# A weight stream split in two parts: the low part of every second chunk by an accumulating transfer

## The chip, the cores and the metric

The kernel runs on one core of one Trainium2 chip. The metric is the device time of one execution in microseconds. A profile of one execution stands beside it; all times in this text come from that profile or from the timed runs.

## What is computed

One layer of a decoder block for 256 tokens of width 2048, in float32: a norm, one wide projection, two branches (dilated attention, a gated recurrence), a gated merge, a mixing product with a norm and a residual, and a gated feed-forward part with a norm and a residual. Cut to what matters:

```python
D_MODEL, SEQ, D_FF = 2048, 256, 5632
a = rmsnorm(x, norm_mix_pre)
proj = a @ w_in                                   # 2048 x 17408
q_a, k_a, v_a, q_r, f_r, i_r, g_r, gate_a, gate_r = split_columns(proj)
attn = ...    # three groups of 8 heads, windows of stride 1, 4, 16, mixed by their denominators
r_out = ...   # HGRN2: S_t = diag(f_t) S_{t-1} + k_t v_t^T, o_t = S_t^T q_t; norm; gate
y = sigmoid(gate_a) * (attn @ w_attn_branch) + sigmoid(gate_r) * (r_out @ w_hgrn_branch)
h = x + rmsnorm(y @ w_mix_out, norm_mix_post)
a = rmsnorm(h, norm_ffn_pre)
gt, up = split(a @ w_ffn_gate_up)                 # 2048 x 11264
out = h + rmsnorm((silu(gt) * up) @ w_ffn_down, norm_ffn_post)
```

## The kernel before

All weights pass through one stream of 600 chunks in the order of the products. A chunk is a tile of 128 partitions by 1024 float32, 512 KB. The products are done at near float32 precision on TensorE by splitting each operand in two parts: a high part, which is the number rounded to TensorE's float32r format, and a low part, which is what the rounding left. Three products (high by high, high by low, low by high) make one.

For each chunk j there are four steps:

1. `load(j)` (L191) issues the transfer from HBM into a tile `raw` on the queue of SP, the sync engine. There are six `raw` buffers.
2. `split(j)` (L206) makes `wh` on ScalarE, a copy that rounds (L221), and then `wl = raw - wh` on VectorE (L222). `wh` and `wl` have three buffers each, except for the last four chunks (`HELD`), which have tiles of their own.
3. `multiply(j)` (L224) issues the matrix products of the chunk on TensorE into `acc` banks of PSUM, of which there are four; a block of columns uses two. It comes in three kinds: N with the activations stationary, T and W with the weights stationary.
4. After the last chunk of a block, its evacuation (`evac`) is put in a queue. It is a generator that is advanced by one step per chunk, on ScalarE, VectorE and partly GpSimd.

The order of the instructions on each engine is the order in which they are written; no scheduler moves them. The main loop (L1116) does for each chunk i: `split(i + 2)`, `load(i + 8)`, `multiply(i)`, and then one step of the evacuations and of two lanes of side work. The lanes hold the attention heads, the recurrence and the second norm. So a split is written two chunks ahead of its use, and the buffers that it writes are those that chunk i - 1 has used last.

GpSimd's queue holds the recurrence's products and differences (L605, L612, L635, L643, L663, L666, L676, L688) and five pieces of the first residual (L874); for the rest of the time it is empty. No transfer is issued on it.

Of the kernel before, what the change touches and what calls it, by code (L numbers as in the profile page):

```python
# [16 lines left out]
AF = mybir.ActivationFunctionType  # L17
OP = mybir.AluOpType
# [18 lines left out]
N_RAW, N_SPLIT, AHEAD, HELD, WARM, BRIDGE = 6, 3, 2, 4, 8, 6  # L37


class Block:  # L40
    """Columns of one product: how they are computed, their operands, and what follows.

    N: 512 columns, activations stationary: tokens on partitions, one bank for 128 tokens.
    T: 512 columns, weights stationary: columns on partitions, two times 128 of them a bank.
    W: 256 columns, weights stationary, both parts of the activations in one stream: 128
       columns a bank, whose halves have yet to be added.
    """

    def __init__(self, kind, w, nk, col, xs, evac, parity=False, pre=None, mid=None, post=None):
        self.kind, self.w, self.nk, self.col = kind, w, nk, col  # L50
# [9 lines left out]
def tile_hybrid_block(ctx: ExitStack, tc: tile.TileContext, t, out):  # L60
    nc = tc.nc
# [3 lines left out]
    stream = ctx.enter_context(tc.tile_pool(name="stream", bufs=1, reuse_waits="tile"))  # L65
# [25 lines left out]
        nc.tensor.matmul(ps, lhsT, rhs, start=start, stop=stop, skip_group_check=True)  # L91

    def rsqrt_mean(dst, ss, n, bias=None):
        """dst = (ss / n + bias) ** -0.5, with a Newton step behind the tables.

        bias: columns with the bias and with -0.5 times it.
        """
        w = ss.shape[-1]
        v, y, a = (small(s)[:, :w] for s in ("v", "y", "a"))
        bias = bias or (eps[:, 0:1], eps[:, 1:2])  # L100
        nc.scalar.activation(y, ss, AF.Ln, scale=1.0 / n, bias=bias[0])
        nc.scalar.activation(y, y, AF.Exp, scale=-0.5)
        nc.vector.tensor_scalar(v, ss, -0.5 / n, bias[1], op0=OP.mult, op1=OP.add)
        if w == 1:
            nc.vector.scalar_tensor_tensor(out=a, in0=y, scalar=v, in1=y, op0=OP.mult, op1=OP.mult)
        else:
            nc.vector.tensor_mul(a, y, y)
            nc.vector.tensor_mul(a, a, v)
        nc.vector.scalar_tensor_tensor(
            out=dst, in0=a, scalar=1.5, in1=y, op0=OP.add, op1=OP.mult  # L110
        )

# [1 line left out]
    warm = cpool.tile([P, 512], mybir.dt.bfloat16, name="warm")  # L114
    nc.vector.memset(warm, 0.0)
    ones = cpool.tile([P, P], F32, name="ones")
# [38 lines left out]
    lb = kp.tile([P, 8], F32, name="lb")  # L155
    lb1 = kp.tile([P, 8], F32, name="lb1")

# [1 line left out]
    blocks, chunks = [], []  # L159

    def add(*args, **kw):
# [23 lines left out]
        return go  # L185

    def parts(j):
        """The first chunk goes in two parts: the arithmetic starts sooner."""
        return (slice(0, 512), slice(512, 1024)) if j == 0 else (slice(0, 1024),)

    def load(j):  # L191
# [14 lines left out]
    def split(j, only=None):  # L206
        if j >= len(chunks):
            return
        raw = chunks[j][2]
        if chunks[j][3] is None:  # L210
            if j < len(chunks) - HELD:
                chunks[j][3:] = [
                    stream.tile([P, 1024], F32R, tag=s, bufs=N_SPLIT, name=nm(s))
                    for s in ("wh", "wl")
                ]
            else:
                chunks[j][3:] = [rslot(s) for s in ("wh", "wl")]
        wh, wl = chunks[j][3:]
        for n, k in enumerate(parts(j)):
            if only in (None, n):  # L220
                nc.scalar.activation(wh[:, k], raw[:, k], AF.Copy)  # L221
                nc.vector.tensor_sub(wl[:, k], raw[:, k], wh[:, k].bitcast(F32))  # L222

    def multiply(j, sides=(0, 1)):  # L224
        b, c = chunks[j][:2]
# [30 lines left out]
                    mm(ps, h, xl, False, False)  # L256
                    mm(ps, l, xh, False, last)

# [1 line left out]
    class Split:  # L260
        """Two K-tiles a slot, each with its high and low part for the 256 tokens."""

        def __init__(self, s, nk, slot=rslot):
            self.flat = [slot(s) for _ in range(nk // 2)]
# [8 lines left out]
            return self(k)[0].bitcast(F32)  # L273

        def put(self, n, src):
            """Both K-tiles of slot n from [128, 2, 256]."""
            x = self.slots[n]
            nc.scalar.activation(x[:, :, 0, :], src, AF.Copy)
            nc.vector.tensor_sub(x[:, :, 1, :], src, x[:, :, 0, :].bitcast(F32))

    def transpose_in(src, gcol, dst, c, apart=False):
        """Two K-tiles of dst from [token, feature] pieces, times a gain by feature."""
        ps = []
        for k in (2 * c, 2 * c + 1):
            if apart or not ps:
                bank = aux()
            ps.append(bank[:, :S] if apart else bank[:, (k % 2) * S : (k % 2 + 1) * S])
            for b in range(2):
                nc.tensor.transpose(  # L289
                    ps[-1][:, b * P : (b + 1) * P],  # L290
                    src[k // 4][:, b, (k % 4) * P : (k % 4 + 1) * P],
                    ident,
                )
        def high(kk):
            k = 2 * c + kk
            nc.scalar.activation(dst(k)[0], ps[kk], AF.Copy, scale=gcol[:, k : k + 1])  # L296

        def low(kk):
            k = 2 * c + kk
            nc.vector.scalar_tensor_tensor(  # L300
                out=dst(k)[1], in0=ps[kk], scalar=gcol[:, k : k + 1],
                in1=dst.f32(k), op0=OP.mult, op1=OP.subtract,
            )

        if apart:
            return high, low
        high(0), high(1), low(0), low(1)

    def row_broadcast(dst, rc):
        """dst[p, t] = rc[t % 128, t // 128] for every p."""  # L310
        ds = [small("diag", P, 2) for _ in range(2)]
        for b in range(2):
            nc.vector.tensor_scalar(ds[b], ident, rc[:, b : b + 1], None, op0=OP.mult)
        yield
        ps = aux()
        for b in range(2):
            mm(ps[:, b * P : (b + 1) * P], ones[:, :P], ds[b], True, True)
        yield
        nc.scalar.activation(dst, ps[:, :S], AF.Copy)
# [16 lines left out]
        while q:  # L336
            advance(q)

# [1 line left out]
    xt = [hslot("x") for _ in range(4)]  # L340
    xv = t["x"][0].rearrange("(b p) c -> p b c", p=P)
    xT = Split("xT", KD)
# [67 lines left out]
        nc.sync.dma_start(lmask, t["lmask"])  # L410

    def keep_warm(n):
        """Products of no use, so that the tensor engine's clock doesn't fall in a wait."""
        ps = aux()
        for _ in range(n):
            mm(ps, warm[:, :P], warm, True, True)
# [15 lines left out]
        if c + 2 < KD // 2:  # L432
            transpose_in(xt, colg, xT, c + 2)

# [1 line left out]
    fT, qT, gN, iN = {}, {}, {}, {}  # L436

    def evac_f(half):
# [60 lines left out]
    qkT, vN = {}, {}  # L499

    def evac_rope(key, tab, then=None):
        """Rotary positions; the tokens leave with the even ones before the odd ones."""
        cos = tabs[:, tab, :]
        sin = tabs[:, tab + 1, :]

# [19 lines left out]
                then()  # L525
        return ev

# [1 line left out]
    attnT = Split("attnT", 8)  # L529
    recT = Split("recT", 8)  # L530

# [44 lines left out]
        )  # L576
        yield

# [1 line left out]
    def recurrence(half):  # L580
        q, f, g = qT[half], fT[half], gN[half]
        q = q.rearrange("p h t -> p (h t)")
# [44 lines left out]
            )  # L627

        def level64():
            """64 tokens against the 64 before them."""  # L630
            x = fslot("x")
            xe, be, ke, qe = (
                a.rearrange("p (e c t) -> p e c t", e=8, c=2) for a in (x, b, kk, q)
# [18 lines left out]
            )  # L652

        def level128():
            """The second 128 tokens against the first."""
            x = fslot("x")
            xc, bc = (a.rearrange("p (h c t) -> p h c t", h=4, c=4) for a in (x, b))
            end = small("end")
# [24 lines left out]
            nc.scalar.activation(a2[0], ps, AF.Copy)  # L683

        def same():
            """A token against itself."""
            x = fslot("x")
            nc.gpsimd.tensor_mul(x, q, kk)  # L688
            yield
# [63 lines left out]
            recT.put(2 * half + j, ps.rearrange("p (h t) -> p h t", h=2))  # L753
            yield

# [1 line left out]
    gates = {}  # L757
    waiting, heads_done = [], [False]

# [26 lines left out]
    part = {}  # L786
# [20 lines left out]
            yT[0].put(2 * j + i, src)  # L807
        return ev

# [1 line left out]
    zg, hx, gpost, zss = {}, {}, [], []  # L811
    h_t, hT = {}, []

# [39 lines left out]
        )  # L853

    def so_far(ss):
        """By side: mean plus eps of the first three of four parts, and -0.5 times it."""
        b = small("base")
        nc.vector.tensor_reduce(
            b[:, :2], ss.rearrange("p (b j) -> p b j", b=2)[:, :, :3], op=OP.add,
# [29 lines left out]
        residual_of(2, False)  # L889

    def residual_of(m, spread=True):
        """The columns behind the K-tiles of chunk m."""
        residual(m // 2, m % 2 * 256, m % 2 * 256 + 256, spread=spread)

    def mid_ffn():
# [78 lines left out]
    def act(k):  # L974
        return act_t[k // 2](k % 2)

# [1 line left out]
    fss, fz, fpost = [], {}, []  # L978

    def begin_down():  # L980
# [40 lines left out]
        return zpool[0].tile([P, 2, 512], F32, tag="z", bufs=4, name=nm(s))  # L1021

    def finish(i):
        """The last tokens of side i: norm, residual, store."""
        sq, r3 = fss[0][:, 4 * i + 3 : 4 * i + 4], r3c[:, i : i + 1]

        def store(j, lo=0, hi=512, eng=nc.sync):
# [13 lines left out]
        down_side(3, i, blocks[-1].banks[i], others)  # L1041
        store(3)

# [1 line left out]
    w_in = t["w_in"][0]  # L1045

    def start_recurrence():
# [97 lines left out]


def _tables():
    """Rotary tables and masks: they depend on shapes alone."""
    inv = (10000.0 ** (-np.arange(0, HD, 2) / HD)).astype(np.float32)
    ang = (np.arange(S, dtype=np.float32)[None, :] * inv[:, None]).astype(np.float64)  # L1150
    cos, sin = np.cos(ang), np.sin(ang)
# [4 lines left out]
    j = np.arange(P)  # L1156
# [31 lines left out]
```

## Time and profile before

| | |
|---|---|
| runs | 1780.1 and 1778.14 us, median 1779.12 |
| span of the profiled execution | 1779.4 us |
| TensorE busy, with 9579 products | 1764.4 us (99%) |
| VectorE busy, 1331 instructions | 1098.2 us (62%) |
| ScalarE busy, 1166 instructions | 846.8 us (48%) |
| GpSimd busy, 54 instructions | 74.1 us (4%) |
| moved by the DMA engines | 326.08 MB, on average 183 GB/s |
| share of the 16 DMA engines taken by SP's queue | 55.6% |

The profiled execution's span is within 0.3 us of the median of the runs, so its rows can be summed against the time directly. In the profile, busy times are sums of instructions by engine; "idle before, releaser" is the time an engine stood idle ahead of a group of instructions and what ended that idle time; the time to landing of a transfer runs from its issue to the arrival of its data.

### The profile page before, as it was taken

The numbers are of one execution on the slowest core, as the hardware profiler recorded it, in microseconds if no ns is written. First come the engines' busy times: TensorE is split into PE (matmuls) and PEld (weight loads), VectorE is DVE, ScalarE is ACT, GpSimd is POOL, SyncE is SP. The second block draws the span as 40 slices with busy tenths as digits, with TensorE's granted clock in tenths as the row PEclk, the third lists the DMA queues.
The fourth block names the chain that finished last, engine by engine and source line by source line (L and its number), as shares of the span: only waits on it lengthen the run. The fifth ranks groups of instructions, "written<-read, shape, count | busy, mean of one in ns | idle before, by whom it ended". The sixth has DMA issues, their size and how long they took to land.

```text
span 1779.4 us, 24318 instructions
## 1 busy us (share of the span) xinstructions
PE 1764.4 (99%) x9579; PEld 1517.8 (85%) x9580; DVE 1098.2 (62%) x1331; ACT 846.8 (48%) x1166; POOL 74.1 (4%) x54
## 2 busy tenths in 40 slices
PE   9999999999999999999999999999999999999998
PEld 7888888888888888888888888888888888888886
DVE  5657658877447775555775576566555566544454
ACT  6545445444444444454554474444444444443443
POOL 0002404300000000000000000000000000000000
PEclk9999999999999999999999999999999999999999
DMA  8656444456445555456557645655566665655553
GB/s 277 196 188 190 133 163 154 151 169 188 155 154 178 190 189 165 155 176 189 191 190 260 200 156 181 187 185 184 187 189 189 188 185 185 213 196 193 192 196 121
DMA packets 268818, 326.08 MB, mean 183 GB/s; under 512 B 10096, under 2 KB 212000, under 8 KB 268704
## 3 DMA queue, kind: packets, MB, share of 16 engines
q1 hardware_dynamic: 266432, 319.41, 55.6%
q10 hardware_dynamic: 2272, 5.12, 0.8%
q8 instruction: 75, 1.23, 0.3%
q14 instruction: 39, 0.32, 0.1%
HBM read 322.40 MB, written 2.10 MB: 182 GB/s over the span
## 4 chain that ended last, share of the span: by engine, by line
PE 98%; DVE 1%; DMA 0%; ACT 0%; issue 0%; POOL 0%; SPq 0%; ACTq 0%
PE acc L91 94%; PE aux L91 4%; PE aux L559 0%; PE aux L289 0%; DMA x<-in_x 0%; DVE x L611 0%; DVE fz L1029 0%; POOL x L605 0%; DVE b L597 0%; ACT wh L221 0%; PE aux L750 0%; SPq L203 0%; ACT junk L1005 0%; ACT junk L838 0%; DVE fz L1008 0%
## 5 line engine op out<-in xcount | busy, mean ns | idle before, releaser
L222 DVE TENSOR_TENSOR wl<-raw,wh 128x1024 fp32r<-128x1024 f32 (+1 forms) x601 | 747.5, 1245 | 641.8 <-ACT wh L221 639.7
L221 ACT ACTIVATE wh<-raw 128x1024 fp32r<-128x1024 f32 (+1 forms) x601 | 634.8, 1058 | 782.9 <-PE acc L91 720.6
L91 PE MATMUL acc<-xT,wh 128*128 128x512 f32 x1536 | 541.4, 398 | 0.0
L91 PE MATMUL acc<-hT,wh 128*128 128x512 f32 (+1 forms) x1472 | 499.3, 389 | 0.4 <-ACT hT L296 0.3
L91 PE MATMUL acc<-xT,wl 128*128 128x256 f32 x1536 | 428.7, 279 | 0.0
L91 PE MATMUL acc<-hT,wl 128*128 128x256 f32 x1408 | 395.5, 281 | 0.0
L91 PEld LDWEIGHTS acc<-xT,wh 128*128 128x128 f32 x1536 | 289.0, 188 | 67.7
L91 PEld LDWEIGHTS acc<-hT,wh 128*128 128x128 f32 x1472 | 272.4, 188 | 63.9 <-ACT hT L296 0.5
L91 PEld LDWEIGHTS acc<-xT,wl 128*128 128x128 f32 x1536 | 290.0, 189 | 0.1
L91 PEld LDWEIGHTS acc<-hT,wl 128*128 128x128 f32 x1408 | 266.1, 189 | 0.0
L91 PE MATMUL acc<-wh,act 128*128 128x512 f32 x704 | 217.0, 389 | 0.0
L91 PE MATMUL acc<-wh,xT 128*128 128x512 f32 x640 | 209.8, 401 | 0.0
L91 PEld LDWEIGHTS acc<-wh,act 128*128 128x128 f32 x704 | 132.1, 188 | 27.4
L91 PEld LDWEIGHTS acc<-wh,xT 128*128 128x128 f32 x640 | 124.1, 194 | 25.2
L91 PE MATMUL acc<-wl,act 128*128 128x512 f32 x352 | 136.9, 389 | 0.0
L91 PE MATMUL acc<-wl,xT 128*128 128x512 f32 x320 | 126.9, 397 | 0.0
L177 DVE TENSOR_TENSOR sum<-acc,sum 128x256 f32<-128x256 f32 x212 | 79.3, 415 | 0.0
L91 PE MATMUL acc<-wh,yT 128*128 128x512 f32 x256 | 79.0, 389 | 0.0
L91 PEld LDWEIGHTS acc<-wl,act 128*128 128x128 f32 x352 | 66.1, 188 | 13.7
L91 PEld LDWEIGHTS acc<-wl,xT 128*128 128x128 f32 x320 | 62.1, 194 | 11.7
L175 ACT ACTIVATE sum<-acc 128x256 f32<-128x256 f32 x212 | 67.7, 371 | 0.0
L91 PEld LDWEIGHTS acc<-wh,yT 128*128 128x128 f32 x256 | 48.0, 188 | 10.0
(189 smaller groups left out, 1077.0 us busy)
## 6 DMA issues: line engine op xcount, KB each, us to landing
raw<-in_w_in SPq DMA_DIRECT2D x271, 512.0 KB, 3.5
raw<-in_w_ffn_gate_up SPq DMA_DIRECT2D x176, 512.0 KB, 4.5
raw<-in_w_ffn_down SPq DMA_DIRECT2D x88, 512.0 KB, 4.5
raw<-in_w_mix_out SPq DMA_DIRECT2D x32, 512.0 KB, 4.3
raw<-in_w_attn_branch SPq DMA_DIRECT2D x16, 512.0 KB, 4.6
raw<-in_w_hgrn_branch SPq DMA_DIRECT2D x16, 512.0 KB, 4.7
hx<-in_x ACTq DMA_DIRECT2D x4, 512.0 KB, 9.8
x<-in_x SPq DMA_DIRECT2D x3, 512.0 KB, 10.8
```

Of the source, the lines that this page charges most:

```text
L91: nc.tensor.matmul(ps, lhsT, rhs, start=start, stop=stop, skip_group_check=True)
L175: nc.scalar.activation(s[:, n, :], ps[:, S:], AF.Copy)
L177: nc.vector.tensor_add(s[:, n, :], ps[:, :S], s[:, n, :])
L221: nc.scalar.activation(wh[:, k], raw[:, k], AF.Copy)
L222: nc.vector.tensor_sub(wl[:, k], raw[:, k], wh[:, k].bitcast(F32))
```

## The change

For every odd chunk j with 2 < j < 596, that is for 297 of the 600, `split` no longer uses VectorE. ScalarE writes the rounded value with its sign turned, `-round(raw)`, into `wl`. Then a transfer on GpSimd's queue adds the tile `raw` to it, from SBUF to SBUF, so that `wl` holds `raw - round(raw)` as before. Then ScalarE writes `wh`. The other chunks are split as before. The rest of the diff removes comments and docstrings and leaves blank lines in their place, so that the lines ahead of this place keep their numbers.

```diff
         wh, wl = chunks[j][3:]
+        if by_dma(j) and only is None:
+            nc.scalar.activation(wl, raw, AF.Copy, scale=-1.0)
+            nc.gpsimd.dma_start(wl, raw, accum_op=OP.add)
+            nc.scalar.activation(wh, raw, AF.Copy)
+            return
         for n, k in enumerate(parts(j)):
             if only in (None, n):
                 nc.scalar.activation(wh[:, k], raw[:, k], AF.Copy)
                 nc.vector.tensor_sub(wl[:, k], raw[:, k], wh[:, k].bitcast(F32))
+
+    def by_dma(j):
+
+        return j % 2 == 1 and 2 < j < len(chunks) - HELD
```

## The prediction

> **What bounds the kernel now.** I read the page's busy times first, then the chain that ended last, then the groups of instructions, then the waits.
>
> ```profile
> span 1779.4 us, 24318 instructions
> PE 1764.4 (99%) x9579; PEld 1517.8 (85%) x9580; DVE 1098.2 (62%) x1331; ACT 846.8 (48%) x1166; POOL 74.1 (4%) x54
> ...
> PEclk9999999999999999999999999999999999999999
> ...
> q1 hardware_dynamic: 266432, 319.41, 55.6%
> ...
> PE 98%; DVE 1%; DMA 0%; ACT 0%; issue 0%; POOL 0%; SPq 0%; ACTq 0%
> ```
>
> TensorE is busy for 1764.4 of 1779.4 us and holds 98% of the chain. Only 15 us are left in which it is idle. VectorE, whose work the change takes away, has 38% of the span free and 1% of the chain. So no edit to VectorE's load can give more than about 15 us; the question is whether the new way of making `wl` still delivers it in time.
>
> ```profile
> L222 DVE TENSOR_TENSOR wl<-raw,wh 128x1024 fp32r<-128x1024 f32 (+1 forms) x601 | 747.5, 1245 | 641.8 <-ACT wh L221 639.7
> L221 ACT ACTIVATE wh<-raw 128x1024 fp32r<-128x1024 f32 (+1 forms) x601 | 634.8, 1058 | 782.9 <-PE acc L91 720.6
> ...
> L222 DVE TENSOR_TENSOR wl<-raw,wh x601: 679/1225/3416, 6.7 to 1757.4; 128x1024 fp32r<-128x1024 f32 x150, 128x512 fp32r<-128x512 f32 x1
> ```
>
> (The last line is the view of the instructions on `wl`: min/median/max ns, first and last start.) These lines carry the argument. ScalarE's idle time before L221 ends on TensorE: `wh` and `wl` have three buffers each, so the split of chunk j starts when TensorE has finished chunk j-3. It must be done when TensorE starts chunk j, and in between TensorE multiplies only chunks j-2 and j-1. The 601 instructions are 600 chunks, since chunk 0 goes in halves; 599 spacings in 1757.4 - 6.7 us are 2.92 us each, so the budget from release to use is B = 5.85 us on average. In the mixing product it is the least:
>
> ```profile
> 999.05 1.06 ACT L221 ACTIVATE wh<-raw 128x1024 fp32r<-128x1024 f32 x1 [1.66 <-PE acc L91]
> ...
> 1000.15 1.23 DVE L222 TENSOR_TENSOR wl<-raw,wh 128x1024 fp32r<-128x1024 f32 x1 [1.49 <-ACT wh L221]
> ...
> 1001.77 1.06 ACT L221 ACTIVATE wh<-raw 128x1024 fp32r<-128x1024 f32 x1 [1.66 <-PE acc L91]
> ```
>
> There a chunk takes 2.72 us, so B is 5.44. The split takes 1.06, a hop of 0.04 (999.05 + 1.06 = 1000.11 to 1000.15) and 1.23, together 2.33 us. It is done 3.1 us early. That slack is all that hides the present way.
>
> **What the change removes and adds.** It concerns the odd chunks from 3 to 595 (HELD = 4 of 600 are left out): 297.
>
> Removed: 297 x 1.245 = 370 us of VectorE, and 1.27 us (0.04 + 1.23) from each chain. Worth nothing directly, since VectorE is not what TensorE waits for; at most it gives back a part of the 15 us.
>
> Added on ScalarE: 297 activations of 1.058 = 314 us, to 1161 us. They stand under the 782.9 us for which L221 waits. `wh` of an odd chunk now comes second, at 2.12 us plus hops after the release, still under 5.44; the even chunk's chain keeps its 2.33. What is queued behind (evacuations of `acc`, which has four banks for two in use) is late by about one microsecond in every second chunk. I cost this at nothing; without that cover each pair would pay up to 1.06, 314 us.
>
> Added on GpSimd's queue: 297 transfers of 512 KB, each waiting for ScalarE. TensorE now waits for the landing. The new latency is L = 1.06 + W + hops, with W from the transfer's issue on GpSimd to its landing. I allow 0.12 for three hops of 0.04, so L = W + 1.18. No row shows an accumulating transfer, so W is bounded by the others:
>
> ```profile
> raw<-in_w_in SPq DMA_DIRECT2D x271, 512.0 KB, 3.5
> raw<-in_w_ffn_gate_up SPq DMA_DIRECT2D x176, 512.0 KB, 4.5
> ...
> out_dram<-fz SPq DMA_DIRECT2D x4, 256.0 KB, 2.2
> ...
> out_dram<-fz SPq DMA_DIRECT2D x2, 64.0 KB, 1.7
> ...
> L203 SPq DMA_DIRECT2D raw<-in_w_in x273: 367/368/1067, 1.2 to 827.7; - x137
> ...
> DMA to landing us min/median/max: 3.3/4.2/11.7
> ```
>
> The stores give a fixed part and a slope: 0.5 us per 192 KB, so 1.53 us for none and 2.87 us for 512 KB. An accumulating transfer must read its destination too, 1 MB in and 512 KB out. The low end is the store's slope with the second read free: 2.9. With the second read paid on that slope it is 1.53 + 2 x 1.33 = 4.2; but those stores ran when hardly any load was left, while these transfers share the 16 engines with the weight stream (55.6% busy). The weight loads are the nearest rows in size and company. Those of `w_in` land after 3.5, of which 2.0 above the fixed part; doubled, 1.5 + 4.0 = 5.5. Those of the gate and up weights land after 4.5, so 1.5 + 6.0 = 7.5. I take 5.5, for the source here is a whole row of 4 KB in SBUF and not a strided one in HBM.
>
> To that comes what GpSimd needs to build the descriptors in excess of SP's 0.37:
>
> ```profile
> L688 POOL TENSOR_TENSOR x<-q,kk 128x1024 f32<-128x1024 f32 x2 | 6.8, 3382 | 0.0
> ...
> L589 POOL MEMSET at<- 128x1024 f32 x2 | 1.9, 952 | 0.0
> ```
>
> Low end nothing, high end its longest operation, 3.4; I take 0.95, the lightest pass over a tile of 128 rows. So W = 6.45 (2.9 to 10.9) and L = 7.63 (4.1 to 12.1).
>
> **From lateness to time.** If TensorE starts odd chunk k late, the buffer for odd chunk k+2 has long been released, since that hung on the even chunk before. So a lateness isn't paid in each pair. With e(k) the end of the even chunk before odd chunk k, its start is the later of e(k) and e(k-1) + L, and e(k+1) is that start + B. For L above B this settles at (L + B)/2 per pair: pairs of B and of L take turns, and the stall of L - B comes at every second odd chunk, about 148 times. The cost is 297 x (7.63 - 5.85)/2 = 264 us. At the low end, L below 5.44, it is nothing; at the high end 297 x 6.25/2 = 928 us.
>
> **GpSimd's own work.** In the recurrence the queue has other work and waits:
>
> ```profile
> 160.00:175.00 15.00, 14.66 (x72) 12.08 (x71) 11.73 (x7) 8.81 (x12) 7.89 (x4) 1.00 0.60 187
> 175.00:380.00 205.00, 203.59 (x1140) 176.55 (x1140) 146.62 (x157) 96.07 (x155) 59.63 (x34) 0.98 0.47 151
> ...
> POOL x L612 <- ACT x L609: 36.4, 12, 6.9
> ...
> POOL x L643 <- ACT x L640: 21.3, 2, 11.5
> ```
>
> (Stages: us, then busy time and count of PE, PEld, DVE, ACT and POOL, clock, DMA share, GB/s.) Of 220 us GpSimd is busy 67.5, in 38 operations of 1.8 us, and 58 us more it waits on ScalarE in 14 waits of 4.1. Some 32 transfers fall in this stretch. With a chance of 0.31 one meets an operation, half of it left (0.3 us); with 0.26 a wait, half of it left (0.5). Half of 0.8 x 32 is 13 us. The other way round, a recurrence operation queued behind a transfer waits for ScalarE's `wl`, whose release came a chunk earlier; at most one issue, at nothing.
>
> SP's load into the same `raw` buffer waits for the landing (at 7.6 us after the release, not 2.3). The load then lands at 7.6 + 4.2 = 11.8; it is needed six chunks after the release, at 17.5. Nothing, unless it takes the longest 11.7.
>
> **Sum.** 1779.4 + 264 + 13 = 2056 us; the span (1779.4) lies 0.3 above the median of the runs, 1779.12, so I give 2056.
>
> Two sentences stand by themselves. By the Trainium skill, DMA: Bandwidth & Descriptors, section "Anatomy of one DMA — SWDGE (gpsimd) path", a GpSimd transfer takes about 2.0 us plus its bytes at 436 GB/s, here an estimate of 3.2 us, which gives L = 4.4 and no cost at all: that is the first rival. Against it speaks the skill's Collectives: The Full Stack, section "The bandwidth ceiling: the fold count and why AG ≠ RS ≠ AR": an add within the transfer halves the rate, for both operands are read on the same side; an estimate by both is 4.4 us, L = 5.6, a few microseconds in the shortest stages only. No run here shows either yet.
>
> **Rivals.**
>
> 1. Hidden, the other side: the landing comes within the budget, and the time is not above the present. Its point is W = 4.26 where B is 5.44 (4.67 at the mean). For it: the stores' slope with two reads gives 4.2, just under it. Against it: the loads of the gate and up weights need 4.5 with one read already. The time is 1779, or down to 1764 + a few if VectorE's relief removes TensorE's last waits. Up to L = 6.1 it stays within 2% (36 us = 297 x 0.24/2).
>
> 2. The 16 DMA engines become the bound. The loads hold 55.6% x 1779.4 / 609 = 1.62 us of all engines each, 3.25 per pair. Two passes for the accumulation add 3.25: 6.5 per pair, less than the 6.74 that I forecast, so it doesn't bind. At three passes (both reads and a write, one after the other, or an adder at that rate) it is 8.1, and the time 1779 + 297 x 2.26 = 2450. For it: the engines are the only resource beside TensorE above half. Against it: an engine that reads and writes at once doesn't pay three passes.
>
> 3. Stalls that lower TensorE's clock. In the opening, with its waits, the granted clock is 0.94:
>
> ```profile
> 0.00:30.00 30.00, 26.67 (x116) 19.88 (x117) 16.28 (x25) 18.39 (x36) 2.81 (x12) 0.94 0.85 298
> ```
>
> At 0.94 throughout, 1764 becomes 1877: 113 us on top of the forecast, 2170. Against it: the short waits about 160 to 175 left it at 1.00.
>
> **How the numbers follow.** Forecast (late by 1 to 3 us, with or without rival 3): 0.56; clock lowered, 0.04 besides; hidden or nearly: 0.20; DMA engines bound or slower still: 0.18; faster by more than the 15 us that are there: 0.02. A measurement of this kernel can tell about 2% (36 us) from no change. The range reaches from the hidden case, 1778, to the engine-bound one, 2450, and leaves out some 0.15, most of it above. The forecast's own range is 1830 to 2300 (W 5.2 to 8.3). Faster by 2% 0.02, within 2% 0.20, slower 0.78.
>
> **What would show it.** Right: L222 falls to 304 instructions, and new ScalarE rows of 1.06 us write `wl`; the waits list TensorE on a DMA to `wl`, about 148 times, each L - B, about 1.8 us; the time to landing of these transfers is near 6.5. Wrong: a time to landing under 4.3 and no TensorE wait (hidden), or a DMA share near 1 with the loads' own landing grown far beyond 4.5 (engine-bound), or stalls at each of the 297 (another buffer holds the chain).

## The result, and the profile after

The changed kernel takes 2265.6 us in the median of two runs (2255.08 and 2276.11), against 1779.12 before: a ratio of 1.273, with a 95% interval of 1.267 to 1.280. The profiled execution has a span of 2253.3 us.

From the page of the changed kernel, the busy times and the DMA queues, and then from the view of the cores (span and mean granted clock), the changed kernel first and then the kernel before:

```profile
span 2253.3 us, 25324 instructions
PE 1901.6 (84%) x9580; PEld 1584.7 (70%) x9580; DVE 747.3 (33%) x1034; ACT 1123.3 (50%) x1463; POOL 322.1 (14%) x351
q1 hardware_dynamic: 266432, 319.41, 44.8%
q0 software_dynamic: 42768, 155.73, 37.9%
core 0: 2253.3 us, clock 0.951
core 0: 1779.4 us, clock 0.996
```

VectorE and ScalarE moved as the diff says: 351 us less on the one, 277 us more on the other. The time went to TensorE. Its idle time (span less busy) grew from 15.0 to 351.7 us. It also lost clock: 2253.3 x 0.049 = 110 us, against 1779.4 x 0.004 = 7 before.

The waits of the changed kernel (who waited for whom; us in total, times, the longest), and the landing of the new transfers and of the loads (KB, median us from issue):

```profile
PEld acc L91 <- DMA wl<-raw: 405.3, 194, 6.5
PE acc L91 <- DMA wl<-raw: 339.1, 182, 6.1
SPq L203 <- DMA wl<-raw: 1589.3, 292, 10.2
wl<-raw POOLq DMA_DIRECT2D x297, 512.0 KB, 6.0
raw<-in_w_in SPq DMA_DIRECT2D x271, 512.0 KB, 5.3
DMA to landing us min/median/max: 4.5/6.0/10.1
```

TensorE stops for one thing, a transfer into `wl`, 194 times. SP, too, now waits for the same landings, since a transfer's end is what frees the `raw` tile of an odd chunk. So one load or two leave SP when a transfer lands (two behind 171 of the 297), and share the engines with the next one. The 161 transfers with two loads issued close to their own issue, from 2.5 us before it to 1.5 us behind, took 7.23 us to land on average, the other 136 took 5.32.

A stretch of ScalarE's timeline in the feed-forward part (start, us, instruction, idle before and its releaser) shows the rhythm; the lines are those that write `wl` for a transfer, the others are left out:

```profile
1441.42 1.06 ACT L220 ACTIVATE wl<-raw 128x1024 fp32r<-128x1024 f32 x1 [1.17 <-PE acc L91]
...
1449.16 1.06 ACT L220 ACTIVATE wl<-raw 128x1024 fp32r<-128x1024 f32 x1 [1.24 <-PE acc L91]
...
1454.81 1.06 ACT L220 ACTIVATE wl<-raw 128x1024 fp32r<-128x1024 f32 x1 [1.84 <-PE acc L91]
...
1463.39 1.06 ACT L220 ACTIVATE wl<-raw 128x1024 fp32r<-128x1024 f32 x1 [1.29 <-PE acc L91]
...
1469.04 1.06 ACT L220 ACTIVATE wl<-raw 128x1024 fp32r<-128x1024 f32 x1 [1.56 <-PE acc L91]
```

The spacings are 7.74, 5.65, 8.58 and 5.65 us: two chunks of TensorE's own pace alternate with a spacing as long as the latency. That is the rhythm of the law in the prediction.

What a stall does to the clock shows in the table by stages (us, busy time and count of PE, PEld, DVE, ACT, POOL, then the clock, DMA share, GB/s), around one stall of the changed kernel:

```profile
330.00:333.50 3.50, 0.20 (x1) 0.20 (x2) 0.00 (x0) 0.86 (x1) 0.87 (x1) 1.00 1.07 272
333.50:337.00 3.50, 3.50 (x9) 2.73 (x9) 0.00 (x0) 0.00 (x0) 0.00 (x0) 0.51 0.90 227
337.00:340.00 3.00, 3.00 (x14) 2.48 (x14) 1.14 (x1) 2.01 (x2) 0.00 (x0) 1.00 0.58 180
```

TensorE stood still, and for the next 3.4 us it ran at half clock: 9 products where the 3 us behind hold 14. Counted over the trace, a stretch at half clock sets in during or just behind 30 of the 33 stalls of 3 us or more, 20 of the 42 from 2 to 3 us, and 6 of some 100 under 2 us. A stretch of 3.4 us costs about 1.7 us on top of the stall.

### The profile page after: what moved, and what is told of

The parts are those of the page before. It is cut to its first block, busy times and chain, and to the rows that moved or that the text cites. A ratio compares the mean times of both kernels' runs of the same rounds, so it can differ in the third digit from the quotient of the medians.

```text
span 2253.3 us, 25324 instructions
## 1 busy us (share of the span) xinstructions
PE 1901.6 (84%) x9580; PEld 1584.7 (70%) x9580; DVE 747.3 (33%) x1034; ACT 1123.3 (50%) x1463; POOL 322.1 (14%) x351
## 3 DMA queue, kind: packets, MB, share of 16 engines
q0 software_dynamic: 42768, 155.73, 37.9%
## 4 chain that ended last, share of the span: by engine, by line
issue 78%; PE 7%; DMA 7%; POOL 6%; ACT 1%; DVE 1%; POOLq 0%; SPq 0%; ACTq 0%; DVEq 0%
PE acc L91 6%; DMA wl<-raw 6%; POOL wl L221 6%; PE aux L91 1%; ACT wl L220 1%; DMA raw<-in_w_mix_out 0%; DMA x<-in_x 0%; POOLq L221 0%; DVE fz L1038 0%; PE aux L298 0%; DVE wl L227 0%; SPq L203 0%; ACT wh L226 0%; ACT wh L222 0%; POOL x L685 0%
## 5 line engine op out<-in xcount | busy, mean ns | idle before, releaser
L227 DVE TENSOR_TENSOR wl<-raw,wh 128x1024 fp32r<-128x1024 f32 (+1 forms) x304 | 377.4, 1242 | 1331.8 <-ACT wh L226 1331.8
L226 ACT ACTIVATE wh<-raw 128x1024 fp32r<-128x1024 f32 (+1 forms) x304 | 320.9, 1056 | 631.7 <-issue 548.8
L91 PE MATMUL acc<-xT,wh 128*128 128x512 f32 x1536 | 569.5, 410 | 0.0
L91 PE MATMUL acc<-xT,wl 128*128 128x256 f32 x1536 | 450.7, 293 | 103.0 <-DMA wl<-raw 102.8
L221 POOL DMA_DIRECT2D wl<-raw x297 | 258.0, 869 | 1879.9 <-ACT wl L220 1817.6
L91 PE MATMUL acc<-hT,wh 128*128 128x512 f32 (+1 forms) x1472 | 519.0, 398 | 0.4 <-ACT hT L305 0.3
L91 PE MATMUL acc<-hT,wl 128*128 128x256 f32 x1408 | 411.9, 293 | 109.0 <-DMA wl<-raw 109.0
L220 ACT ACTIVATE wl<-raw 128x1024 fp32r<-128x1024 f32 x297 | 313.7, 1056 | 364.0 <-PE acc L91 358.9
L222 ACT ACTIVATE wh<-raw 128x1024 fp32r<-128x1024 f32 x297 | 309.3, 1042 | 0.0
L91 PE MATMUL acc<-wh,act 128*128 128x512 f32 x704 | 230.8, 411 | 0.0
```

The source lines that it names most:

```text
L220: nc.scalar.activation(wl, raw, AF.Copy, scale=-1.0)
L221: nc.gpsimd.dma_start(wl, raw, accum_op=OP.add)
L222: nc.scalar.activation(wh, raw, AF.Copy)
```

## The experiments

Theory A was lateness: a transfer's latency L, from ScalarE's start of `wl` to the landing, against a budget of two chunks. Theory B was throughput: the DMA engines, now 83% busy, set the pace. Means of L and of the landing are counted over all transfers of the trace; for the changed kernel they are 7.82 and 6.35 us. Where a ratio is given below the kernel ran four times; the others ran once. The four runs of `e6_half` lie 27 us apart, so a difference of that size between two single runs says little by itself.

**Four buffers for `wl`** (`e1_wl4`):

```diff
-N_RAW, N_SPLIT, AHEAD, HELD, WARM, BRIDGE = 6, 3, 2, 4, 8, 6
+N_RAW, N_SPLIT, AHEAD, HELD, WARM, BRIDGE = 5, 3, 2, 4, 8, 6
-    stream.tile([P, 1024], F32R, tag=s, bufs=N_SPLIT, name=nm(s))
-    for s in ("wh", "wl")
+    stream.tile([P, 1024], F32R, tag=s, bufs=n, name=nm(s))
+    for s, n in (("wh", N_SPLIT), ("wl", N_SPLIT + 1))
```

> Four buffers for wl instead of three, five for raw instead of six; all else as in the changed kernel. ScalarE can now start an odd chunk's wl one chunk earlier, so the budget from release to use grows from two chunks (5.85 us) to three (8.8 us). Theory A (lateness: the latency from ScalarE's start to the landing, 7.8 us on average, against the budget): nearly all landings come in time, TensorE's idle time falls from 339 us to under 50, the half clock with it, and the time is 1780 to 1850 us. Theory B (throughput: the 16 DMA engines, 83% busy, set the pace): buffers don't help, above 2100 us.

Measured: 2119 us (ratio to before 1.193, 1.189 to 1.197), between what the two theories gave. ScalarE's timeline shows why:

```profile
1424.62 1.06 ACT L226 ACTIVATE wh<-raw 128x1024 fp32r<-128x1024 f32 x1 [3.43 <-PE acc L91]
1425.59 0.64 ACT L175 ACTIVATE sum<-acc 128x256 f32<-128x256 f32 x2
1428.42 0.63 ACT L971 ACTIVATE sig<-g 128x512 f32<-128x512 f32 x1 [2.20 <-DVE g L970]
1428.96 1.05 ACT L220 ACTIVATE wl<-raw 128x1024 fp32r<-128x1024 f32 x1
```

The odd chunk's `wl` (L220) has its buffer, but it stands in order behind the even chunk's `wh` (L226), which waits for TensorE, and behind evacuations. Both buffers came free with the same chunk, at about 1424.6, and 4.3 of the 8.8 us were gone before `wl` started. That is a bad case, with an evacuation's wait of 2.2 us in it. Over all transfers `wl` started on average 1.06 us ahead of the release on which it had hung with three buffers, out of the 2.9 us that a fourth buffer offers. The edit didn't give the budget that I had counted on, so it decided nothing; the run `e5_early` below does.

**No loads** (`e2_noloads`): in `load`, `if j > 23: chunks[j][2] = chunks[j - N_RAW][2]; return`.

> Leaves out every weight load from chunk 24 on; the chunks then use the six raw tiles that are there, so the values are not the reference's, and the instructions on all engines but SP stay the same. It takes the other traffic off the DMA engines. Theory A1 (the transfer's own latency is what is late): issue to landing falls little, 5.5 to 6.3 us on average instead of 6.35, and the time stays above 2100 us. Theory A2 (the transfer is late because it shares the engines with the loads): issue to landing falls to about its present minimum of 4.5 us, the latency from ScalarE's start to 6.0, and the cost to 297 x (6.1 - 5.85)/2 = 40 us, so 1800 to 1850 us.

Measured: 1937 us. From the issues and the page of this run:

```profile
wl<-raw POOLq DMA_DIRECT2D x297, 512.0 KB, 4.5
PE 1814.9 (94%) x9580; PEld 1524.1 (79%) x9580; DVE 749.9 (39%) x1034; ACT 1122.0 (58%) x1463; POOL 325.1 (17%) x351
```

The landing fell from 6.35 to 4.77 us on average, as A2 said: the loads make 1.6 us of it. The time is some 90 us above A2's range. TensorE's idle time grew by 105 us over before, where I had expected 40: L (6.23 on average) is still above the budget, and the mean budget of 5.85 hides that most pairs have less. Another 14 us are clock, and 36 us are what I put down to the restart of a stopped TensorE; I had priced neither (below).

**A plain copy** (`e3_plain`): `accum_op=OP.add` taken away.

> The same transfer without the addition: wl then holds a copy of raw, so the low parts of these chunks are wrong; all instructions and their order stay. If the second read is what costs (two reads for one write), the share of the engines per transfer falls from 2.87 to about 1.5 us, issue to landing from 6.35 to about 4.7 us, the latency to 6.2, and the time to 1830 to 1900 us. If the addition costs nothing, and GpSimd's way of issuing is what is slow, it stays above 2150 us.

Measured: 2035 us, between the two ranges.

```profile
q0 software_dynamic: 42768, 155.73, 22.3%
wl<-raw POOLq DMA_DIRECT2D x297, 512.0 KB, 5.0
```

The share per transfer is 22.3% x 2033 / 297 = 1.53 us of all engines, against 37.9% x 2253.3 / 297 = 2.87 with the addition. So the addition nearly doubles the work of the engines, but only 1.3 us of the landing come with it (6.35 to 5.03 on average); the rest is paid by a plain copy too.

**The same copy from ScalarE's queue** (`e8_plain_act`): `nc.scalar.dma_start(wl.bitcast(F32), raw)`.

> The plain copy of the run before (low parts of these chunks are wrong), issued by ScalarE's queue instead of GpSimd's. On GpSimd the issue takes 0.87 us and starts 0.40 us after ScalarE's end, and the copy lands 5.0 us after its issue began. If GpSimd's way of issuing costs about a microsecond, the latency from ScalarE's start to the landing falls from 6.5 to about 5.7 us and the time from 2035 to about 1880 us, though ScalarE now waits for its own result before each issue. If the queue makes no difference, 2000 to 2060 us.

Measured: 2002 us, at the edge of the second case.

```profile
wl<-raw ACTq DMA_DIRECT2D x297, 512.0 KB, 5.1
```

The copy lands 5.1 us after its issue there, 5.0 from GpSimd, so GpSimd's queue is not what makes a plain copy's landing late. What is saved is the hop: 0.40 us from ScalarE's end to the issue on GpSimd, 0.05 on ScalarE's own queue. The two single runs differ by 33 us. The accumulating transfer was not tried from this queue.

**The transfer one chunk earlier** (`e5_early`), with four `wl` buffers and five `raw` buffers as in `e1_wl4`:

```diff
+    def low_early(j):
+        if by_dma(j):
+            tiles(j)
+            nc.scalar.activation(chunks[j][4], chunks[j][2], AF.Copy, scale=-1.0)
+            nc.gpsimd.dma_start(chunks[j][4], chunks[j][2], accum_op=OP.add)
...
+        low_early(i + AHEAD + 1)
         split(i + AHEAD)
```

> The run with four wl buffers left ScalarE's order as it was: an odd chunk's wl stands behind the even chunk's wh, which waits for TensorE itself, so only a part of the third chunk was won. Here the same buffers, and an odd chunk's wl and its transfer are written one chunk earlier, ahead of that wh. The budget from release to use is now 8.8 us, the latency some 7.9 us. Theory A (lateness): idle time falls below 100 us. But each pair asks 2 x 1.66 us of all 16 DMA engines for its loads and 2.87 us for its transfer, 6.2 us against 5.85 us of TensorE, so theory B takes over as a floor: 1779 + 297 x 0.35 = 1880 us. Expected 1870 to 1960 us with the DMA share above 0.9. If lateness were not the cause of the idle time, it stays near the 2119 us of the run with four buffers.

Measured: 1834.5 us, 1.031 of before (1.029 to 1.033).

```profile
PE 1779.6 (97%) x9580; PEld 1522.8 (83%) x9580; DVE 754.8 (41%) x1034; ACT 1128.9 (62%) x1463; POOL 319.9 (17%) x351
q1 hardware_dynamic: 266432, 319.41, 51.4%
q0 software_dynamic: 42768, 155.73, 46.4%
PEld acc L91 <- DMA wl<-raw: 40.3, 38, 3.3
```

The same 297 transfers, no sooner landed (6.62 us on average), now cost 55 us instead of 486: 38 stalls instead of 194. Theory A is shown: against `e1_wl4`, only the place of `wl` and its transfer in the order has changed. It came out below my floor of 1880, since the loads take 51.4% x 1832.4 / 609 = 1.55 us of the engines here, not 1.66; with that the floor is about 1812. What is left fits theory B, with the engines 98% busy, but 56 transfers still land later than 8.8 us after `wl` starts, so it is not shown which of the two it is.

**Half of the columns** (`e6_half`): the transfer makes `wl[:, :512]`, VectorE the rest.

> The transfer makes only the first 512 columns of wl; VectorE makes the others. Half the bytes: issue to landing about 3.5 us, the latency from ScalarE's start to the landing about 5.0 us, less than the shortest budget of 5.44, and 4.8 us of DMA engine time per pair. Theory A: hidden, 1778 to 1800 us. If the cost of a transfer doesn't go by its bytes but by its issue and its landing, issue to landing stays above 5 us and the time above 1900.

Measured: 2009 us (1.125, 1.120 to 1.131), where I had expected it hidden. The landing took 5.20 us on average, not 3.5. **Without the loads** (`e10_half_noloads`) the same transfer was tried again:

> The half transfer with three buffers, and every weight load from chunk 24 on left out (the chunks use the raw tiles that are there, so the values are not the reference's). With the loads, half the bytes took 5.2 us to land, against a minimum of 3.24. If the loads in front make the difference, issue to landing is 3.2 to 3.4 us, the latency 4.3 to 4.5, below every budget, and the time is 1775 to 1795 us. If the half transfer is slow by itself, issue to landing stays near 5 us and the time near 2000.

Measured: 1814 us. The landings of the two runs, then TensorE with the loads left out:

```profile
wl<-raw POOLq DMA_DIRECT2D x297, 256.0 KB, 5.2
wl<-raw POOLq DMA_DIRECT2D x297, 256.0 KB, 3.3
PE 1778.2 (98%) x9579; PEld 1521.5 (84%) x9580; DVE 957.4 (53%) x1331; ACT 997.1 (55%) x1463; POOL 327.9 (18%) x351
```

With the loads away it lands in 3.3 us, as expected, and the loss is nearly gone; the time is some 20 us above the range that I gave. Of the 19 us of idle time that stay, some 8 belong to the first 24 chunks, whose loads were kept. Four landings now give an estimate of the terms: 3.3 and 4.5 us in the median without loads for 256 and 512 KB, 5.2 and 6.35 on average with them. So a fixed 2.05 and 1.25 per 256 KB, a line through two sizes, and 1.6 to 1.7 for the loads (the averages without loads are 3.50 and 4.77), about the same for both sizes. Both sizes go in the same number of packets (42768), so whatever a packet costs is in the fixed part. Halving the bytes takes away 1.15 of 6.35 us and leaves the other two terms.

**Fillers** (`e7_filler`): ahead of the products of chunk j, `if j % 4 == 1 and by_dma(j): keep_warm(12)`.

> The changed kernel with 12 products of no use (0.21 us each, 2.6 us) ahead of the products of every fourth chunk, so that TensorE is busy where it would stand still. Theory A with the clock as a term of its own (some 200 us more at half clock, that is 102 us of the 486): the fillers take the place of the stalls, the half clock falls from 222 to under 80 us, idle time from 339 to under 80 us, and the time is 2120 to 2200 us in spite of 148 x 2.6 = 380 us of added products. If the half clock costs nothing, the fillers only replace idle time and the time stays at 2250 or rises.

Measured: 2317 us.

```profile
core 0: 2314.8 us, clock 0.989
PE 2187.8 (95%) x11356; PEld 1697.7 (73%) x11356; DVE 741.1 (32%) x1034; ACT 1124.5 (49%) x1463; POOL 323.2 (14%) x351
```

The clock came back, as expected: 2314.8 x 0.011 = 25 us lost instead of 110. The time did not; it rose, which by the expectation's own words is the case of a half clock that costs nothing. The terms say otherwise. The fillers follow one another after 0.216 us, so they cost 1776 x 0.216 = 384 us, and they took away 225 us of idle time (351.7 to 127.0), less than I had hoped. If nothing else had changed, 384 - 225 would have put this span at 2412 us; it is at 2315. The 85 us of clock are most of that difference. This is an account from one run; what half clock does to the products is seen directly in the table by stages above.

**One transfer in four chunks** (`e4_every4th`): `j % 4 == 3` in `by_dma`.

> Only every fourth chunk by transfer (148 instead of 297), the others by VectorE. Theory A with its law (L + B)/2: when every odd chunk is transferred, each stall gives the next transfer the time that it lacks, so only every second one stalls; with one in four there is a full pair in between, each stalls by L - B, and the number of stalls stays near 148 to 175. With a latency of 7.3 to 7.8 us the idle time is 148 x 1.5 to 2.0 = 220 to 300 us, the half clock stays near 200 us, and the time is 2050 to 2200 us. Rival (every transfer costs the same share): half of the 486 us, 2020 us, with about 88 stalls.

Measured: 1975 us, below both.

```profile
wl<-raw POOLq DMA_DIRECT2D x149, 512.0 KB, 4.7
PEld acc L91 <- DMA wl<-raw: 178.2, 123, 6.4
```

My ranges had taken the latency of the full traffic; with half the transfers it fell to 6.44 us. So the two kernels don't differ in one thing only, and the count of stalls (123 of 149, where the changed kernel has 194 of 297) is all that speaks for the law. The run was repeated **without the loads** (`e11_4th_noloads`), where the latency is the same with 297 and with 149 transfers (6.0 us in the median of both):

> Every fourth chunk by a full transfer, loads from chunk 24 on left out as before. With the loads out, the latency is that of the run without loads (6.0 us in the median, 6.2 on average), so the number of transfers alone is changed. There 297 transfers cost TensorE 105 us of added idle time. By the law (stalls of (L - B)/2 per odd chunk when all odd chunks are transferred, of L - B when every second one is) half the transfers cost about the same: 80 to 110 us of idle time, 0.6 to 0.7 per transfer, time 1890 to 1935 us. By equal shares it is half: 50 us, time 1850 to 1860 us.

Measured: 1926 us, against 1937 with twice as many.

```profile
span 1924.3 us, 23345 instructions
PE 1812.9 (94%) x9579; PEld 1530.8 (80%) x9580; DVE 929.4 (48%) x1182; ACT 983.0 (51%) x1315; POOL 200.5 (10%) x203
```

Idle time is 111.4 us, against 1935.2 - 1814.9 = 120.3. Over the 15.0 of before that is 96 us, in the range by the law and twice what equal shares give. Half the transfers, nearly the same loss: that is the law, and equal shares are out.

**Early and half** (`e9_early_half`): the early kernel with the half transfer.

> The early kernel (four wl buffers, the transfer written one chunk earlier, ahead of wh) with the half transfer: 512 columns by transfer, 512 by VectorE. Latency about 6.3 us against a budget of 8.8, and 4.8 us of DMA engine time per pair against 5.85. Theory A: hidden entirely; TensorE's idle time is back near 15 us and the half clock near 18 us, and the time is 1772 to 1785 us: relief of VectorE by 140 us is worth nothing, since TensorE didn't wait for it. If VectorE's relief were worth something, it is below 1765.

Measured: 1798.6 us, 1.011 of before (1.009 to 1.013). The last two lines are TensorE's waits for VectorE in the recurrence, in this run and in the kernel before:

```profile
PE 1770.7 (99%) x9579; PEld 1523.3 (85%) x9580; DVE 954.6 (53%) x1331; ACT 997.5 (56%) x1463; POOL 322.6 (18%) x351
PEld acc L91 <- DMA wl<-raw: 3.4, 2, 1.8
PE aux L91 <- DVE x L628: 8.6, 4, 4.9
PE aux L91 <- DVE x L611: 1.6, 2, 1.3
```

The transfers are hidden (2 stalls), VectorE has 144 us less to do, and nothing is gained: the kernel is 1.1% slower, less than the 2% that the prediction counts as a difference, but outside what I had expected. About 11 us of it are idle time, 7 of them waits in the recurrence, and about 7 us are clock. No version tried beats the kernel before.

## Why the prediction was right, and where it was short

The direction, the mechanism and the range held, but the range was wide (1778 to 2450) and the sum was short: the loss was 474 us between the profiled executions and 277 in the sum. Three measures close the account: idle time above the 15.0 us of before, clock lost above 7, and the number of stalls. The run with fillers is left out, since its added products are in its span.

| run | span over before | idle | clock | rest | stalls |
|---|---|---|---|---|---|
| the change | 473.9 | 336.7 | 103 | 34 | 194 |
| `e1_wl4` | 321.1 | 234.4 | 60 | 27 | 146 |
| `e3_plain` | 253.6 | 178.6 | 38 | 37 | 168 |
| `e6_half` | 236.1 | 158.7 | 43 | 34 | 147 |
| `e8_plain_act` | 220.7 | 155.7 | 33 | 32 | 147 |
| `e4_every4th` | 193.3 | 135.9 | 28 | 29 | 123 |
| `e2_noloads` | 155.8 | 105.3 | 14 | 36 | 168 |
| `e11_4th_noloads` | 144.9 | 96.4 | 22 | 27 | 122 |
| `e5_early` | 53.0 | 37.8 | 9 | 6 | 38 |
| `e10_half_noloads` | 32.4 | 18.6 | 6 | 8 | 40 |
| `e9_early_half` | 17.6 | 11.3 | 7 | -1 | 2 |

One transfer in the timelines of ScalarE and GpSimd, for the second point below:

```profile
1499.88 1.06 ACT L220 ACTIVATE wl<-raw 128x1024 fp32r<-128x1024 f32 x1 [1.17 <-PE acc L91]
1501.34 0.86 POOL L221 DMA_DIRECT2D wl<-raw  x1 [3.25 <-ACT wl L220]
```

Point by point:

- **The landing**, W: 6.45 forecast, 6.35 on average. The size was right, its parts only by luck. I had doubled a load's time above a fixed part; by the estimate above it is 2.05 fixed, 2.5 for 512 KB and 1.6 for the loads' company (medians and a difference of averages, so the sum is 6.15). The descriptor building that I added (0.95) did not show as a cost beside a hardware queue's: a plain copy from ScalarE's queue lands no sooner.
- **The hops**: 0.12 for three, but ScalarE's end to GpSimd's start alone takes 0.40 (1499.88 + 1.06 = 1500.94 to 1501.34). With that, L is 7.82 on average, 7.63 forecast.
- **The law**: (L + B)/2 was right in kind. With the measured L it gives 297 x (7.82 - 5.85)/2 = 293 us; TensorE's added idle time is 337. I had 264 + 13. It also gave about 148 stalls, and there are 194. The shortfall comes from taking one L and one B for all. B is a mean that 38 long pairs with side work, up to 10.5 us, pull up; three quarters of the pairs take 5.66 us or less. L runs from 5.9 to 11.5. Followed chunk by chunk, with each transfer's own landing and TensorE's pace of before, the law gives 369 us and 189 stalls here, 117 us in `e2_noloads` (measured 105), 136 in `e4_every4th` (136) and 94 in `e11_4th_noloads` (96). The 13 us for the recurrence could not be seen apart.
- **SP's loads at nothing**: wrong in one way. The loads arrive in time, as said, but they leave at the landings, often in pairs, and lengthen the next transfer. Taking the loads out takes 1.6 us off the landing.
- **The step that failed**: the clock stood among the rivals, with 113 us and a chance of 0.04 of its own, because short waits in the kernel before had left it at 1.00. It belongs in the sum: 103 us. The stalls of before were no longer than 2.2 us; here 33 reached 3 us. The kernel before had given a hint: its clock was at half for 3.4 us at 9.6 and at 310.0 us, 1 to 2 us behind idle times of 2.1 and 1.3 us.
- **Not in the working at all**: the restart of TensorE. The rest column is 0.16 to 0.24 us per stall in all runs but the last, which has only two. A product of 512 columns lasts 0.39 us by itself, and the next one starts 0.23 us behind it; a stop loses that overlap of 0.16, which would explain most of it. No run tested this.

By the Trainium skill, TensorE: Matmul & The Clock Gate, section "HAM oscillation — how this bites in real kernels", a wait for data that outlasts the clock gate's activity window makes TensorE start again at the lower clock; this trace agrees (3.4 us at half clock with 30 of 33 stalls of 3 us or more). The section puts the limit at gaps of about 3.4 us; here 20 of 42 stalls of only 2 to 3 us brought half clock too, and the trace decides. The two sentences of the prediction on transfers gave 4.4 us together; the run without loads has 4.5, so they fit a transfer that has the engines to itself, and the measured 6.35 beside the loads decides here.

The first rival (hidden) fell at W = 6.35. The second (engines bound) was not the case here, at 83%; it may be what is left in the early kernel, at 98%. The third (a lower clock) came true, with about its size.

## What to carry to other kernels

Ask first what the engine that you relieve is holding up: VectorE held up nothing, so all that a slower way could do was arrive late. A chain that is hidden by slack has to be costed as a latency from the release of its buffer to its use, chunk by chunk and not by means, its landing taken beside the traffic that its own completion lets loose, and a fixed part (here some 2 us) counted before any bytes. Once TensorE stops, add to the stall what it brings with it: here about 0.2 us of restart each, and a stretch of 3.4 us at half clock with half of the stalls of 2 to 3 us and nearly all longer ones.

## What was not expected of the hardware

- Two of the transfers' terms did not shrink when their bytes were halved: about 2.05 us fixed and 1.6 us beside the loads, out of 6.35.
- An accumulating transfer takes 1.9 times the engine time of a copy (2.87 against 1.53 us), but only 1.3 us more to land.
- With a budget of three chunks the DMA engines were at a share of 98%, and the kernel was only 3% slower than before.
